# Three banks for the sums of the long mLSTM scan, one for its transposes, the next head's scores inside the round, and loads of two later stages moved

## The chip, the core and the metric

The kernel runs on one core of a Trainium2 chip, in one launch. A core has a matrix engine (TensorE, "PE" in the profile; its weight loads, which overlap the products, stand as "PEld"), a vector engine ("DVE"), a scalar engine ("ACT"), GpSimd ("POOL") and SyncE ("SP"), from whose queue nearly all DMA transfers of this kernel are issued. Matrix products go to banks of an accumulator memory (PSUM), from which ACT or DVE reads them. The metric is the time of one execution on the device, in microseconds (us).

## The reference

One encoder layer, applied to a long input of 1024 tokens and a short one of 512, both 1024 wide, with the same weights:

```python
h = rms_norm(x, pre_w)
cols = jnp.einsum('bsd,dc->bsc', h, w_in)
m_qk, m_v, m_o, m_z, m_i, m_f, a_qkv, a_z, gate = jnp.split(cols, ...)
y_m = mlstm_mixer(m_qk, m_v, m_o, m_i, m_f, ...) * silu(m_z)
y_a = dilated_attention(a_qkv, rel_table) * silu(a_z)
p_m, p_a = y_m @ w_pm, y_a @ w_pa
g = sigmoid(gate)                       # one gate per branch
merged = g[:, :, 0] * p_m + g[:, :, 1] * p_a
return x + rms_norm(merged @ w_out, post_w)
```

The mLSTM mixer has 4 heads of 256 channels and runs over chunks of 128 tokens, forward and backward; the two directions are added. In one chunk of one direction:

```python
sc = jnp.einsum('nhtk,nhsk->nhts', qc, kc) * jnp.exp(d_log - mt[..., None])
num = jnp.einsum('nhts,nhsv->nhtv', sc, vc) + wa[..., None] * jnp.einsum('nhtk,nhkv->nhtv', qc, c_mat)
h = num / jnp.maximum(jnp.abs(den), jnp.exp(-mt))[..., None]
c_new = decay[..., None, None] * c_mat + jnp.einsum('nhsk,nhsv->nhkv', kw, vc)
```

The attention has three groups (window 128 with stride 1, 512 with stride 4, 2048 with stride 16) of 8 heads of 64 channels. The groups' outputs are mixed, weighted by their softmax denominators.

## The kernel before

Every large product is made in three passes of split numbers: high by high, high by low and low by high (`mm3`, lines 194 to 196, so these three lines stand for most of PE's work). ACT makes the high half of a weight block (`split_w`, L252: `wh<-wraw`) and DVE the low half (L253: `wl`), from one of two buffers `wraw`, into one of three pairs `wh`, `wl`. One such weight block, a "unit" of 128 x 1024, serves 8 or 16 products into the banks called `dense`, three passes each. One `dense` step (called a step below) is one such triple.

The program goes through stages: the values of both inputs, then the projections of the first columns in pairs of units (up to 1056 us), the scan of the long tokens (called A; `mlstm`, to 1353), the attention of A (`attend`, to 1645), the scan of the short tokens (B; `mlstm_short`, to 1833) with the mix of A's three attention groups beside it (`combine` with `slow`), the attention of B (`attend`, to 2122), and a closing stage with the mix of B (`combine` without `slow`). All the other projections are cut into the `dense` steps, and `fill` strews them over the scans, the attentions and the closing stage: `fill(1 / 3)` gives out a third of what a round is due, by a plan that spreads a stage's number of steps (STEPS) over its calls. `fill(lead)` ahead of a stage counts as `lead` calls. The order on PE and on SP is the order of the code in these stages (`manual_schedule`); on ACT, DVE and POOL a scheduler gives the order.

**The scan of A.** `mlstm` runs 64 rounds: 4 heads, 8 chunks (`i`), 2 directions (`d`). Its PSUM pool (L870 to L872) has two banks `a` (transposes and scores), two banks `num` (the sums of a round) and one `kv` of two banks. Ahead of the rounds stand the loads of the first rows and of V, `fill(lead)`, and `prepare(0)`. `prepare(h)` is a generator of six steps for a head: twice a group of scores `a<-Q,K` (L892, 8 products of which each is in two parts, copied by ACT at L894 into `st`) and two groups of transposes of K (L901, copied by ACT at L902 back into `K`). Each takes a bank `a`.

A round `k` does: `tick()` (SP gives out `pace` queued loads and the stores that are due), one step of `prepare` of the next head where one is under way (from `i == 4` of a head on, one a round for six rounds), `rows`, `front(k + 1)` (ACT, DVE and POOL make `rm`, `sch`, `scl`, `qh`, `ql`, `kh`, `kl` for the next round's products), the `turn` of round `k - 4` (PE transposes the normed sum `hn` into a bank `a`, L1005, and DVE multiplies it into `ym`, L1007), a third of the fill, and `core(k)`. `core` multiplies the scores by V into `num`, gives a third of the fill, multiplies K by V into `kv`, a third of the fill, and multiplies `qh`, `ql` by the state `ch`, `cl` into the same `num` (six products). ACT (L990, `X<-num`, in the first four chunks) or DVE (L993, in the last four) then takes `num` over into `hacc` (an array in the buffer `X0`), which frees its bank.

**The attention** goes in 12 units. At each unit's second tile (`j == 1`) the loads of the next are queued (`ready`), and `spread(T.n - 1)` says over how many ticks they are given out; B has `T.n` = 4, A has 8. What is not yet out when the unit begins, `need` gives out at once. The scores are `lg<-V1a,Q` (L1387). In B's units V1a takes the K and Q the queries, from `aqk_b`.

**The mix** (`combine`) has per token block `t` a load of the three groups' outputs into one of two buffers (`load(t)`: `V0a`, `V1a` for B, `V0b`, `V1b` for A), `weigh`, `mix` (reads the buffer for the last time), `add`, and the `turn` of the block before. Its steps are yielded in turn to the loop beside it.

## Time and profile before

| | us |
|---|---|
| median of three runs | 2278.14 (2277.72 to 2280.95) |
| profiled execution, its own time | 2278.09 |
| its span, first to last instruction | 2276.3 |
| PE busy in it | 2235.5 |

By stage, from one answer of the trace in windows:

| stage | window, us | PE busy, us | granted clock |
|---|---|---|---|
| values of both inputs | 0 to 300 | 297.76 | 1.00 |
| pairs of units | 300 to 1056 | 753.77 | 1.00 |
| scan of A | 1056 to 1353 | 282.99 | 0.98 |
| attention of A | 1353 to 1645 | 288.35 | 1.00 |
| scan of B, mix of A | 1645 to 1833 | 186.18 | 1.00 |
| attention of B | 1833 to 2122 | 281.77 | 0.99 |
| closing stage, mix of B | 2122 to 2276 | 144.69 | 0.98 |

A window's length less PE's busy time is what PE stood still in that stage: 14.0 us in the scan of A, 7.2 in the attention of B, 9.3 in the closing stage. The granted clock is TensorE's, as a share of full speed, where 1.00 is no loss; at a lower clock the products themselves take longer, so this loss is inside the busy time. A name in the profile like `a<-Q,K` gives what an instruction writes and what it reads, without the numbers of the buffers; the order below prints some of these numbers (`wh_8712` is one of the three buffers for high halves).

### The profile page before, as it was taken

What the parts mean: (1) busy time and instruction counts of PE and PEld (TensorE: products, weight loads), DVE (VectorE), ACT (ScalarE), POOL (GpSimd) and SP (SyncE); (2) the same over time, 40 slices, a digit from 0 to 9 for tenths busy, and PEclk for the clock granted to TensorE, in tenths of its full rate; (3) what the DMA queues carried; (4) which work ended last, traced back from release to release, by engine and by line L of the source; (5) the groups of instructions that cost most, each with busy time, mean ns of one, the idle gap of its engine ahead of it and who ended that gap; (6) DMA issues with size and microseconds to landing.
All of it is one profiled execution on the core that took longest, in us unless ns stands there. A gap on an engine that the chain in (4) does not pass through costs nothing. (4 is left out here: it accounts for less than half of the span.)

```text
span 2276.3 us, 35152 instructions
## 1 busy us (share of the span) xinstructions
PE 2235.5 (98%) x12210; PEld 1951.7 (86%) x12210; DVE 1467.8 (64%) x2777; ACT 1100.5 (48%) x2255; POOL 623.6 (27%) x801
## 2 busy tenths in 40 slices
PE   9999999999999999999999999999999999999998
PEld 9999998888887888887888889989888878888787
DVE  5587556767899655643787776675477744556563
ACT  7444223434444433334677766676644354544332
POOL 1000023333333322222567640001033321311311
PEclk9999999999999999999999999999999999999999
DMA  9556435555332223424666559988788888787673
GB/s 355 192 138 143 117 113 194 196 193 195 118 111 101 95 82 109 146 97 159 242 214 218 157 164 250 237 234 216 203 240 264 250 259 221 192 261 208 219 248 116
DMA packets 253627, 425.05 MB, mean 187 GB/s; under 512 B 26209, under 2 KB 150753, under 8 KB 252681
## 3 DMA queue, kind: packets, MB, share of 16 engines
q1 hardware_dynamic: 249848, 410.20, 58.7%
q10 hardware_dynamic: 3600, 12.59, 1.4%
q8 instruction: 97, 1.59, 0.3%
q14 instruction: 82, 0.66, 0.1%
HBM read 302.72 MB, written 128.37 MB: 189 GB/s over the span
## 5 line engine op out<-in xcount | busy, mean ns | idle before, releaser
L194 PE MATMUL dense<-H,wh 128*128 128x512 f32 x672 | 280.5, 417 | 0.0
L196 PE MATMUL dense<-H,wl 128*128 128x512 f32 x672 | 265.6, 395 | 0.5 <-DVE wl L253 0.5
L195 PE MATMUL dense<-H,wh 128*128 128x512 f32 x672 | 264.5, 394 | 0.0
L196 PE MATMUL d<-Hh,phla 128*128 128x512 f32 x608 | 237.4, 390 | 2.2 <-DVE phla L538 2.2
L194 PE MATMUL d<-Hh,phla 128*128 128x512 f32 x608 | 236.9, 390 | 0.0
L195 PE MATMUL d<-Hl,phla 128*128 128x512 f32 x608 | 236.8, 390 | 0.0
L195 PE MATMUL d<-vlo,Hh 128*128 128x322 f32 x704 | 220.4, 313 | 0.8 <-DVE vlo L384 0.8
L196 PE MATMUL d<-vhi,Hl 128*128 128x322 f32 x704 | 220.3, 313 | 0.0
L194 PE MATMUL d<-vhi,Hh 128*128 128x322 f32 x704 | 220.3, 313 | 0.0
L253 DVE TENSOR_TENSOR wl<-wraw,wh 128x1024 fp32r<-128x1024 f32 x109 | 137.0, 1257 | 89.8 <-ACT wh L252 87.7
L556 POOL TENSOR_TENSOR psum_w<-pw_raw 128x512 f32<-128x512 f32 x38 | 57.5, 1512 | 445.8 <-DMA pw_raw<-w_in 422.1
L1399 DVE CUSTOM_DVE_ANT_0 ls<-lg,bias 128x256 f32<-128x256 f32 (+1 forms) x288 | 93.7, 362 | 132.7 <-PE lg L1387 68.2
L194 PE MATMUL d<-Hh,phlb 128*128 128x512 f32 x456 | 177.6, 390 | 0.0
L196 PE MATMUL d<-Hh,phlb 128*128 128x512 f32 x456 | 177.6, 389 | 0.0
L195 PE MATMUL d<-Hl,phlb 128*128 128x512 f32 x456 | 177.6, 389 | 0.0
L1403 ACT ACTIVATE ls<-ls,nm 128x256 f32<-128x256 f32 (+1 forms) x288 | 129.9, 453 | 79.6 <-DVE nm L1401 63.1
L252 ACT ACTIVATE wh<-wraw 128x1024 fp32r<-128x1024 f32 x110 | 116.0, 1054 | 85.1 <-DMA wraw<-w_pm 32.8
L196 PEld LDWEIGHTS dense<-H,wl 128*128 128x128 f32 x672 | 126.7, 189 | 29.7 <-DVE wl L253 0.9
L195 PEld LDWEIGHTS dense<-H,wh 128*128 128x128 f32 x672 | 127.8, 190 | 13.6
L194 PEld LDWEIGHTS dense<-H,wh 128*128 128x128 f32 x672 | 127.4, 190 | 13.5
L196 PEld LDWEIGHTS d<-Hh,phla 128*128 128x128 f32 x608 | 114.1, 188 | 27.6 <-DVE phla L538 4.2
L195 PEld LDWEIGHTS d<-vlo,Hh 128*128 128x128 f32 x704 | 133.5, 190 | 1.5 <-DVE vlo L384 1.4
(556 smaller groups left out, 5722.2 us busy)
## 6 DMA issues: line engine op xcount, KB each, us to landing
pw_raw<-w_in SPq DMA_DIRECT2D x76, 512.0 KB
wraw<-w_in SPq DMA_DIRECT2D x76, 512.0 KB
aqk_a<-pwk SPq DMA_DIRECT2D x48, 512.0 KB
aqk_b<-sw SPq DMA_DIRECT2D x48, 256.0 KB
wraw<-w_pm SPq DMA_DIRECT2D x24, 512.0 KB
wraw<-w_out SPq DMA_DIRECT2D x24, 512.0 KB
vb<-w_vp SPq DMA_DIRECT2D x16, 644.0 KB
va<-w_vp SPq DMA_DIRECT2D x14, 644.0 KB
```

What stands on the lines that cost most here:

```text
L194: nc.tensor.matmul(out, lh, rh, start=start, stop=False)
L195: nc.tensor.matmul(out, lh, rl, start=False, stop=False)
L196: nc.tensor.matmul(out, ll, rh, start=False, stop=stop)
L252: self.splits = (nc.scalar.activation(hi[:, :n], raw[:, :n], AF.Copy), on.tensor_sub(lo[:, :n], raw[:, :n], hi[:, :n].bitcast(F32)))
L253: on.tensor_sub(lo[:, :n], raw[:, :n], hi[:, :n].bitcast(F32)))
L556: self.nc.gpsimd.tensor_add(s[:, 0], ws[1][:, 0], ws[1][:, 1])
L1399: nc.vector.tensor_tensor_reduce(out=ls[:, hh], in0=ts["lg"][hh], in1=bt[:, hh], scale=1.0, scalar=NEG, op0=OP.add, op1=OP.max, accum_out= ...
L1403: nc.scalar.activation(ls[:, hh], ls[:, hh], AF.Exp, bias=nm[:, hh:hh + 1], accum_out=ot[:, 128 + hh:129 + hh])
```

## The change

Five things are changed.

- The scan of A has one bank `a` and three banks `num`, in place of two and two.
- A step of the next head's `prepare` is given out inside `core(k)`, after the products into `kv` and their share of the fill, ahead of the six products of `qh`, `ql`. Before, it stood at the round's start, ahead of `rows`, `front` and `turn`.
- The lead of the scan of A is 8 in place of 4.
- In `attend`, B's unit 1 has its loads given out over one tick, in place of three. All others stay.
- `combine` gives out `load(0)` and `load(1)` at its start and `load(t + 2)` after the mix of `t` (beside the scan of B) or after its sum (in the closing stage). Before, `load(t + 1)` stood ahead of block `t`'s work.

```diff
--- before.py
+++ after.py
@@ -868,7 +868,8 @@
         with ExitStack() as stack:
             sb = self.pool(stack, "ml" + T.name, 2, "right")
             ps = self.ml_ps = self.pool(stack, "ml_ps" + T.name, 2, "right", PSUM)
-            bank = {"a": lambda: ps.tile([P, 4, P], F32, name="a"), "num": lambda: ps.tile([P, 512], F32, name="num"),
+            bank = {"a": lambda: ps.tile([P, 4, P], F32, name="a", bufs=1),
+                    "num": lambda: ps.tile([P, 512], F32, name="num", bufs=3),
                     "kv": lambda: ps.tile([P, 2, 512], F32, name="kv", bufs=1)}
             spare = {b: bank[b]() for b in banks}
             psum = lambda b: spare.pop(b, None) if b in spare else bank[b]()
@@ -946,6 +947,8 @@
                     nc.vector.scalar_tensor_tensor(kl, kc, wsc, kh.bitcast(F32), op0=OP.mult, op1=OP.subtract)
                     m["k"] = (kh, kl)
 
+            coming = []
+
             def core(k):
                 h, i, d = rounds[k]
                 x, m = head[h], made.pop(k)
@@ -965,6 +968,8 @@
                     for ct in range(2):
                         self.mm3(pc[:, ct, :258], (kh[:, ct], kl[:, ct]), v, True, True)
                     fill(1 / 3)
+                for x1 in coming:
+                    next(x1, None)
                 if i > 0:
                     qh, ql = m["q"]
                     _, ch, cl = C[d]
@@ -1021,7 +1026,6 @@
             for _ in prepare(0):
                 fill(1 / 3)
             front(0)
-            coming = None
             for k, (h, i, d) in enumerate(rounds):
                 self.tick()
                 if i == (n > 4) and d == (n <= 4):
@@ -1032,9 +1036,7 @@
                         after()
                         self.spread(2 * n - 4)
                 if d == 0 and i == n // 2 and h < 3:
-                    coming = prepare(h + 1)
-                if coming is not None and next(coming, coming) is coming:
-                    coming = None
+                    coming.append(prepare(h + 1))
                 if k % 4 < 2:
                     rows(k // 4 + 1, k % 4)
                 if k + 1 < len(rounds):
@@ -1468,7 +1470,7 @@
                     if j == 1:
                         if i < 11:
                             coming = ready(i + 1)
-                            self.spread(T.n - 1)
+                            self.spread(T.n - 1 if i or T.n > 4 else 1)
                         elif after:
                             after()
                             self.spread(T.n + 1)
@@ -1556,20 +1558,23 @@
             self.put(("ym", T.S, 4), T.ym[8:12, :, t * P:(t + 1) * P].rearrange("c p s -> p c s"), ya, az)
 
         load(0)
+        load(1)
         yield
         az, w = {}, []
         for t in range(T.n):
             az[t] = az_of()
             self.fetch(("az", T.S), az[t].rearrange("p (c s) -> p c s", c=4), T.az[:, :, t * P:(t + 1) * P].rearrange("c p s -> p c s"))
-            if t + 1 < T.n:
-                load(t + 1)
-            for step in (lambda: w.append(weigh(t)), lambda: mix(t, w[t]), lambda: add(t)):
+            for i, step in enumerate((lambda: w.append(weigh(t)), lambda: mix(t, w[t]), lambda: add(t))):
                 with self.tc.issue_after(self.splits[0].ins), self.tc.issue_after(self.splits[1].ins):
                     step()
                 if slow:
                     yield
+                    if i == 1 and t + 2 < T.n:
+                        load(t + 2)
             if not slow:
                 yield
+                if t + 2 < T.n:
+                    load(t + 2)
                 yield
             if t > 0:
                 turn(t - 1, az[t - 1])
@@ -1995,7 +2000,7 @@
                 sraw = sp.tile([P, BLK + 2], F32R, name="sraw")
                 N.sg, N.sraw = Rot(N, [sraw[:, :BLK]]), sraw.bitcast(F32)
                 head = N.ml_load(A, 0)
-                N.mlstm(A, fill, STEPS[0], head, ("a", "num", "kv"), 4,
+                N.mlstm(A, fill, STEPS[0], head, ("a", "num", "kv"), 8,
                         hold("qkv", lambda: N.att_first(A)))
                 with ExitStack() as s3:
                     lanes = N.lanes_short(B, N.pool(s3, "lane2", 1, "right"), lambda: N.bank("o").rearrange("p a b -> p (a b)"))
```

What this does to the order, at three places. The first is PE at the start of the scan of A. Before, the first scores (L892) come behind the last step of the second weight unit that stands ready (`wh_8710`), and its steps go on between the groups of `prepare(0)`:

```order
L196 MATMUL dense<-H_8720,wl_8711 128x512
L194 MATMUL dense<-H_8720,wh_8710 128x512
L195 MATMUL dense<-H_8721,wh_8710 128x512
L196 MATMUL dense<-H_8720,wl_8711 128x512
L892 MATMUL a<-Q_8778,K_8779 128x128 x8
L194 MATMUL dense<-H_8720,wh_8710 128x512
L195 MATMUL dense<-H_8721,wh_8710 128x512
L196 MATMUL dense<-H_8720,wl_8711 128x512
L901 MATMUL a<-ident,K_8779 128x128 x4
L194 MATMUL dense<-H_8722,wh_8710 128x512
L195 MATMUL dense<-H_8723,wh_8710 128x512
L196 MATMUL dense<-H_8722,wl_8711 128x512
```

In the changed kernel the lead goes on through that unit and through six steps of the third, which lies in `wh_8712`, and the scores (now L893) and transposes (L902) stand behind these:

```order
L196 MATMUL dense<-H_8722,wl_8711 128x512
L194 MATMUL dense<-H_8720,wh_8712 128x512
L195 MATMUL dense<-H_8721,wh_8712 128x512
L196 MATMUL dense<-H_8720,wl_8713 128x512
L194 MATMUL dense<-H_8720,wh_8712 128x512
...
L194 MATMUL dense<-H_8722,wh_8712 128x512
L195 MATMUL dense<-H_8723,wh_8712 128x512
L196 MATMUL dense<-H_8722,wl_8713 128x512
L893 MATMUL a<-Q_8778,K_8779 128x128 x8
L902 MATMUL a<-ident,K_8779 128x128 x4
L194 MATMUL dense<-H_8722,wh_8712 128x512
```

The first scores have moved from behind 11 steps of the scan's lead to behind 22, and the last six of these use the third weight unit. ACT's order at the same place, before (`st` and `K` are the copies out of `a`, `wh` the high half of a weight unit):

```order
L938 ACTIVATE qh<-qw 128x256
L894 ACTIVATE st_8794<-a 128x512
L930 ACTIVATE sch<-rm 128x128
L902 ACTIVATE K_8779<-a 128x2x256
L945 ACTIVATE kh<-K_8779,col_382 128x256
L902 ACTIVATE K_8779<-a 128x2x256
L926 ACTIVATE rm<-rm,col_382 128x128
L894 ACTIVATE st_8794<-a 128x512
L252 ACTIVATE wh_8712<-wraw_8706 128x1024
L930 ACTIVATE sch<-rm 128x128
```

And ACT's order in the changed kernel:

```order
L939 ACTIVATE qh<-qw 128x256
L641 ACTIVATE sw_8775<-dense 128x512
L252 ACTIVATE wh_8712<-wraw_8706 128x1024
L252 ACTIVATE wh_8708<-wraw_8707 128x1024
L252 ACTIVATE wh_8710<-wraw_8706 128x1024
L895 ACTIVATE st_8794<-a 128x512
L931 ACTIVATE sch<-rm 128x128
L903 ACTIVATE K_8779<-a 128x2x256
L946 ACTIVATE kh<-K_8779,col_382 128x256
L927 ACTIVATE rm<-rm,col_382 128x128
L903 ACTIVATE K_8779<-a 128x2x256
```

The high half of the third unit, which stood behind both score copies, now stands ahead of both, with those of the two units after it.

The second place is PE in a round of the scan of A in which a `turn` follows a step of the next head's `prepare`, from the six products of `qh`, `ql` on (`ident` is the unit matrix by which PE transposes, `K_9046` the next head's K, `hn_8801` a normed sum):

```order
L194 MATMUL num<-ch_9605,qh 128x258
L195 MATMUL num<-cl_9606,qh 128x258
L196 MATMUL num<-ch_9605,ql 128x258
L194 MATMUL num<-ch_9605,qh 128x258
L195 MATMUL num<-cl_9606,qh 128x258
L196 MATMUL num<-ch_9605,ql 128x258
L901 MATMUL a<-ident,K_9046 128x128 x4
L1005 MATMUL a<-ident,hn_8801 128x128 x2
L194 MATMUL dense<-H_8722,wh_8708 128x512
L195 MATMUL dense<-H_8723,wh_8708 128x512
```

The same round in the changed kernel, where the numbers of the buffers K, `ch` and `cl` differ:

```order
L196 MATMUL dense<-H_8722,wl_8711 128x512
L902 MATMUL a<-ident,K_9085 128x128 x4
L194 MATMUL num<-ch_9645,qh 128x258
L195 MATMUL num<-cl_9646,qh 128x258
L196 MATMUL num<-ch_9645,ql 128x258
L194 MATMUL num<-ch_9645,qh 128x258
L195 MATMUL num<-cl_9646,qh 128x258
L196 MATMUL num<-ch_9645,ql 128x258
L1010 MATMUL a<-ident,hn_8801 128x128 x2
L194 MATMUL dense<-H_8722,wh_8710 128x512
```

The transposes of K have moved from behind the six products to ahead of them; the `turn` follows six products later instead of at once, and both take the one bank `a` where they took one of two. With `d` and `i` as before, each of the first three heads has such places.

The third place is SP at unit 1 of B's attention. Before, from the first of its loads on (`wraw` is a raw weight unit, `ymr` and `sraw` are inputs of a projection, `bias` the bias table, `sw` a result that is stored):

```order
L231 DMA ymr_18367<-ym_a 128x512
L231 DMA Q_18005<-aqk_b 64x512 x2
L231 DMA V1a<-aqk_b 64x512 x3
L210 DMA wraw_8706<-w_pm 128x1024
L231 DMA ymr_18368<-ym_a 128x512
L210 DMA wraw_8707<-w_pm 128x1024
L231 DMA ymr_18369<-ym_a 128x512
L231 DMA V1a<-aqk_b 64x512
L231 DMA Q_18005<-aqk_b 64x512 x2
L231 DMA V1a<-aqk_b 64x512 x2
L210 DMA aqk_b<-sw_8775 128x512
L210 DMA aqk_b<-sw_8776 128x512
...
L231 DMA sraw<-ym_a 128x512
L231 DMA V1a<-aqk_b 64x512 x2
L231 DMA bias_8768<-erep 128x256 x2
```

And in the changed kernel:

```order
L231 DMA ymr_18367<-ym_a 128x512
L231 DMA Q_18008<-aqk_b 64x512 x2
L231 DMA V1a<-aqk_b 64x512 x4
L231 DMA Q_18008<-aqk_b 64x512 x2
L231 DMA V1a<-aqk_b 64x512 x4
L231 DMA bias_8768<-erep 128x256 x2
L210 DMA wraw_8706<-w_pm 128x1024
L231 DMA ymr_18368<-ym_a 128x512
L210 DMA wraw_8707<-w_pm 128x1024
L231 DMA ymr_18369<-ym_a 128x512
L210 DMA aqk_b<-sw_8775 128x512
L210 DMA aqk_b<-sw_8776 128x512
```

All eight loads of `V1a` and four of `Q` now stand together, followed by the bias table's two, ahead of the two weight units `w_pm`, where the last two of `V1a` and the bias table stood behind three weight units and two stores.

## The prediction

> **What bounds the kernel now.** I read the page first, then the list of waits of PE, then the granted clock in windows, and last the timeline around each wait that the change can touch. Of the page, its first line and PE's; of the waits, "engine, line, what it waited for: us in total, times, longest":
>
> ```profile
> span 2276.3 us, 35152 instructions
> PE 2235.5 (98%) x12210; PEld 1951.7 (86%) x12210; DVE 1467.8 (64%) x2777; ACT 1100.5 (48%) x2255; POOL 623.6 (27%) x801
> ...
> PE num L194 <- ACT X L990: 6.8, 6, 2.3
> PE lg L1387 <- DMA sraw<-ym_a: 4.7, 1, 4.7
> PE a L892 <- DMA K<-qk_a: 3.7, 2, 2.3
> PE dense L194 <- DVE mg L1716: 2.4, 1, 2.4
> PE num L194 <- ACT rm L926: 1.3, 1, 1.3
> PE num L194 <- DVE X L993: 0.9, 2, 0.5
> ```
>
> PE is the bound: 2276.3 - 2235.5 = 40.8 us of the span is idle, and the change adds no matrix multiplication and takes none away. Only PE's waits, and what they drag behind them, can move. The largest are the four that the change is near: the sums' banks (`num`, 6.8 + 0.9), the first unit change in the short attention (4.7), the start of the long scan (3.7) and the closing stage (2.4).
>
> A wait also costs something behind it. The windows (length, busy time and count of PE, PEld, DVE, ACT, POOL, then PE's granted clock, DMA share, GB/s) show it:
>
> ```profile
> 1090.00:1100.00 10.00, 6.73 (x38) 5.28 (x38) 7.64 (x16) 6.54 (x18) 6.77 (x10) 0.97 1.00 393
> 1100.00:1110.00 10.00, 10.00 (x55) 8.99 (x54) 7.38 (x15) 6.19 (x15) 4.36 (x10) 0.86 1.03 358
> 1855.00:1865.00 10.00, 5.24 (x20) 4.22 (x20) 2.98 (x8) 5.82 (x14) 3.93 (x6) 0.66 1.02 322
> 1290.00:1300.00 10.00, 10.00 (x55) 8.94 (x55) 6.42 (x16) 6.41 (x17) 4.32 (x7) 0.83 0.90 200
> ```
>
> After a wait of 2.3 us the clock is lowered: 0.03 and 0.14 of two 10 us windows are lost, 1.7 us (0.17 of 10 in the second place, at 1290); after the wait of 4.7 us 0.34 of 10 us, part of it while PE still stood, so about 1.9 us. So **a pause over 2 us costs 1.7 to 1.9 us more**.
>
> The sum below is made against the profiled execution, 2278.09 us (its span 2276.3 and 1.8 around it), which stands at the median of the three runs, 2278.14.
>
> **The start of the long scan: +8.2 us.** Timeline rows are start, duration, engine, line, operation, and in brackets the wait before it:
>
> ```profile
> 1056.51 0.39 PE L194 MATMUL dense<-H,wh 128*128 128x512 f32 x1
> ...
> 1063.76 0.39 PE L196 MATMUL dense<-H,wl 128*128 128x512 f32 x1
> ...
> 1065.62 0.49 PE L892 MATMUL a<-Q,K 128*128 128x128 f32 x2 [1.47 <-DMA K<-qk_a]
> ...
> 1068.37 2.97 PE L892 MATMUL a<-Q,K 128*128 128x128 f32 x14 [2.26 <-DMA K<-qk_a]
> ...
> 1068.71 2.15 SPq L210 DMA_DIRECT2D wraw<-w_in  x2
> ...
> 1077.38 1.06 ACT L252 ACTIVATE wh<-wraw 128x1024 fp32r<-128x1024 f32 x1 [0.22 <-DMA wraw<-w_in]
> ...
> 1079.75 0.50 PE L196 MATMUL dense<-H,wl 128*128 128x512 f32 x1 [0.49 <-DVE wl L253]
> ...
> 1080.78 0.28 PE L194 MATMUL num<-V0a,sch 128*128 128x258 f32 x1
> ...
> 1083.07 1.06 ACT L252 ACTIVATE wh<-wraw 128x1024 fp32r<-128x1024 f32 x1 [1.14 <-DMA wraw<-w_in]
> ```
>
> Now the lead is 11 steps of three products (1056.51 to 1063.99: 0.68 us a step), then the scores wait for K until 1068.37. The change makes it 22 steps, so the wait for K goes. But two units of weights, 16 steps, are ready; they end at 1056.5 + 16 x 0.68 = 1067.4. The third unit's weights are asked of SP at 1068.71, behind the Q, K and V loads, and stay there in the order of after; they land at 1077.4 and their high half is ready at 1078.44. **PE stands from 1067.4 to 1078.5, 11 us**, where it stood 3.7. From there to the first `num` product come 12 steps (8.2), two score groups (16 products each, 2 x 1.70) and four transpose groups (4 x 0.35): 13.0. The low half, ready at 1079.75, holds the first step for 0.8, the lowered clock costs 1.3 (it ran down while PE stood), and the single bank makes five hand-overs in a row, which I put at 2.2: each waits for ACT's copy (0.58), behind which ACT has `sch`, `kh` or `rm` before the next one, against one step of 0.68 as cover. ACT's fourth split, ahead of the score copies now, ends at 1083.07 + 1.06, before they are due. So the first `num` starts at 1078.5 + 13.0 + 0.8 + 1.3 + 2.2 = 1095.8 instead of 1080.78: 15.0 later, of which 10 steps (6.8) are work done ahead. That leaves 8.2; bounds 4.7 (no hand-over waits, no lowered clock) and 11 (twice the clock's loss). The steps moved ahead leave 2.69 a round instead of 2.84, 0.1 us less cover in each round; I count nothing for it, since the rounds between the waits run without a gap.
>
> **The third bank: -7.0 us.** Two waits at a `num` bank, and beside the second what its products need:
>
> ```profile
> 1098.19 0.39 PE L194 MATMUL num<-V0a,sch 128*128 128x258 f32 x1 [2.29 <-ACT X L990]
> ...
> 1288.37 0.45 POOL L931 TENSOR_TENSOR scl<-rm,sch 128x128 fp32r<-128x128 f32 x1
> 1289.58 0.51 ACT L945 ACTIVATE kh<-K,col 128x256 fp32r<-128x256 f32 x1
> 1289.74 0.39 PE L194 MATMUL num<-V1a,sch 128*128 128x258 f32 x1 [2.32 <-ACT X L990]
> ```
>
> With a third bank a round waits for the copy of the round before last, one round (3 to 4 us) earlier. The waits are 6.8 + 0.9 = 7.7, and 3.4 of clock behind the two long ones: 11.1 at most, 0 at least. The wait of 2.29 I take whole, with its clock: 4.0. The one of 2.32 moves: `scl` ends at 1288.82 and `kh` at 1290.09, so the next products stand behind these; 0.5, and half of the clock, 0.9. Of the other 3.1, half, 1.6; together 6.5, and 0.5 for the first rounds, whose loads have 8 us more. What is late next is `scl` on POOL and `kh` on ACT.
>
> **One bank for transposes: +4.5 us.** PE's products into `a`, and ACT's copies out of it:
>
> ```profile
> 1128.25 1.95 PE L892 MATMUL a<-Q,K 128*128 128x128 f32 x16
> 1131.19 0.57 ACT L894 ACTIVATE st<-a 128x512 f32<-128x512 f32 x1
> ...
> 1204.12 0.60 PE L901 MATMUL a<-ident,K 128*128 128x128 f32 x4
> 1206.67 0.58 ACT L902 ACTIVATE K<-a 128x512 f32<-128x512 f32 x1
> ```
>
> In after the scores of the next head stand in front of the six `q` products (0.72), and `turn` of the round behind them. It comes 1.07 us after the transposes begin, or 2.4 after the scores begin; the copies end 3.13 and 3.51 after. In full this is a wait of 2.1 and 1.1. There are three such places in each of three heads: 0 to 13.4 (nine gaps between such rows as they stand now). While PE waits ACT catches up, and only the first of each three is paid nearly whole: 4.5. Behind PE stand the `dense` and `num` products, nothing else.
>
> **Loads of the short attention: -6.0 us.**
>
> ```profile
> V1a<-aqk_b SPq DMA_DIRECT2D x32, 128.0 KB
> ...
> 1848.34 1.06 ACT L252 ACTIVATE wh<-wraw 128x1024 fp32r<-128x1024 f32 x1 [2.96 <-DMA wraw<-w_pm]
> ...
> 1853.70 0.59 ACT L1413 ACTIVATE pts<-pt 128x512 f32<-128x512 f32 x1
> ...
> 1854.11 1.09 SPq L231 DMA_DIRECT2D V1a<-aqk_b  x2
> ...
> 1860.34 1.15 PE L1387 MATMUL lg<-V1a,Q 128*128 128x256 f32 x2 [4.74 <-DMA sraw<-ym_a]
> ```
>
> The scores wait for the last two `V1a` loads, issued at 1854.11 behind a row of stores and weights. (The row names another load that landed with them.) In after all fourteen loads of that unit go out in one turn, ahead of two `wraw` and two `ymr`, so the wait of 4.7 and its 1.9 of clock go: 6.6. Ten loads of 128 KB pushed ahead of `wraw` put it off by some 4 us, so the split of 1848.34 becomes 1852.4, and `pts` behind it 1854.1 to 1854.7, where PE wants it at 1854.31: 0.5 back. Bounds -6.6 and -2 (should a later split block ACT as long again).
>
> **Loads of the mix.** In the closing stage:
>
> ```profile
> V1a<-og_b SPq DMA_DIRECT2D x6, 264.0 KB
> ...
> 2126.00:2128.00 2.00, 2.00 (x11) 1.65 (x10) 1.46 (x2) 0.59 (x2) 0.26 (x1) 1.00 0.98 309
> 2131.05 1.06 ACT L252 ACTIVATE X<-wraw 128x1024 fp32r<-128x1024 f32 x1 [0.71 <-DMA wraw<-w_out]
> 2134.25 1.60 SPq L231 DMA_DIRECT2D V1a<-og_b  x3
> ...
> 2141.61 0.17 DVE L1523 TENSOR_TENSOR cw<-V1a 128x8 f32<-128x8 f32 x1 [2.34 <-DMA V1a<-og_b]
> 2143.41 0.50 PE L194 MATMUL dense<-wh,H 128*128 128x512 f32 x1 [2.38 <-DVE mg L1716]
> ```
>
> DVE stands at the mix's first row behind the load of 2134.25, and PE behind DVE: 2.4, and 1.7 of clock. Moved up, that load goes; but its three parts (264 KB each, 0.81 MB) now lie ahead of the `wraw` that ACT is already waiting for at 2131.05, and at 300 GB/s put it off by 2.7 us: PE then waits about 2.4 there, with half a chance of the clock. Net -1.0, bounds -4.1 and +3. In the mix of the long tokens the loads also move up; the weights there are two units ahead, 16 steps or 11 us, so nothing; without that cover 2.7 us.
>
> **A rule of the skill against this.** The rows above lower the clock after a pause of 2.3 us. The Trainium skill, "TensorE: Matmul & The Clock Gate", its closing table, asks only that idle gaps stay below about 3 us, one idle window of the monitor. The trace differs (2.32 us, clock 0.83 in the ten microseconds after it), so the sum goes by the trace; what the other would give stands below as a rival.
>
> **Sum**: 8.2 - 7.0 + 4.5 - 6.0 - 1.0 = -1.3, so 2278.1 - 1.3 = **2276.8 us**.
>
> **Rivals.**
> - *The single bank is paid in full* (slower). ACT's copy stays as late behind PE as now, each of the nine places costs its gap: 13.4 in place of 4.5, 2285.7 us. It decides from the point where a copy ends later than 1.07 us after its transposes begin. For it: the copy above ends 3.13 after. Against: ACT is busy 48% and gains while PE stands. Chance 0.22.
> - *The scan is freed* (faster). All 11.1 of the bank waits go, and the copies come forward, since the scheduler gives them out anew: 1 in place of 4.5. 2278.1 + 8.2 - 11.1 + 1 - 6.0 - 1.0 = 2269.2. For it: the six bank waits end at one and the same copy. Against: `scl` and `kh` above. Chance 0.30.
> - *The third bank does not do what it says*: the feeders (`kh`, `scl`, `rm`) are late anyway, as 1.3 us of the list already is, and of the 7.0 only 2 come: 2281.8. Chance 0.06.
> - *Short pauses cost no clock*: then the scan gains 4.4 for 7.0, the closing stage 0 for 1.0, and the old pause for K costs 1.7 less, so the start 9.9: 2278.1 + 9.9 - 4.4 + 4.5 - 6.0 = 2282.1. This is the rule named above; against it stands its own row. Chance 0.02.
>
> **The numbers.** The forecast has 0.40. A measurement of this kernel can tell about 0.2%, 4.6 us, from no change: the forecast, the third and the fourth rival lie within, 0.48; the second is faster, 0.30; the first slower, 0.22. The range takes in the centres of both large rivals with a little beyond, 2268 to 2287; the forecast's own, by the bounds of the start and the closing stage, is 2272 to 2282.
>
> **What would show it.** Right: PE's first product of the third unit waits about 11 us on ACT `wh` at the scan's start; `num` waits on ACT `X` fall from 6.8 below 2; `a` <- ident, `hn` (the turn) appears among PE's waits with 3 to 6 us; `lg` no longer waits in the short attention; `dense` waits on ACT or DVE `X` near 2132 instead of on `mg`. Wrong: if the wait at the start is under 6 us, the third unit's load came earlier than its place on SP says; if the turn waits over 10 us, the first rival holds; if `num` waits as before on `kh` or `scl`, the third.

## The result and the profile after

The changed kernel takes 2293.82 us (median of 4 runs, 2288.24 to 2298.39), the kernel before 2278.9 (4 runs, 2277.72 to 2280.95). The ratio is 1.0066, with a 95% interval of 1.005 to 1.0082: 15 us slower, beyond the upper end of the forecast range (2287). The profiled execution of the changed kernel, 2298.39, is the slowest of its four.

The page of the changed kernel, its first line and PE's:

```profile
span 2296.6 us, 35144 instructions
PE 2241.6 (98%) x12210; PEld 1952.5 (85%) x12210; DVE 1469.4 (64%) x2777; ACT 1101.2 (48%) x2255; POOL 617.5 (27%) x801
```

PE has the same 12210 products and stands still for 55.0 us, where it was 40.8. Its busy time is 6.1 us longer with the same work, which is lowered clock. PE's list of waits (engine, line, what it waited for: us in total, times, longest):

```profile
PE dense L194 <- ACT wh L252: 10.9, 1, 10.9
PE dense L194 <- DVE H L1657: 4.1, 1, 4.1
PE kv L194 <- DVE cf L985: 3.2, 5, 1.4
PE a L1010 <- ACT K L903: 3.0, 5, 1.2
PE a L1010 <- ACT st L895: 3.0, 3, 1.7
PE o L1424 <- ACT ot L1426: 2.5, 3, 1.0
...
PE dense L194 <- ACT X L252: 1.8, 1, 1.8
```

The waits at `num`, at `lg` and at K, the three largest before, are gone. In their place stand one of 10.9 us for the third weight unit, 6.0 of the turn at the one bank `a`, and three kinds that were not there or were small: `kv`, `o`, and in the closing stage X and H.

Where the two profiles part, by the first row of each stage on PE (us; the last column is what the stage added):

| from | to | before | after | added |
|---|---|---|---|---|
| first step of the lead | first product into `num` | 24.3 | 40.3 | 16.0, of which 6.8 is work done ahead: 9.2 |
| first product into `num` | first `lg` of A's attention | 271.1 | 264.8 | -6.3 + 6.8 = 0.5 |
| first `lg` | last `lg` of A's attention | 293.2 | 297.8 | 4.6 |
| last `lg` of A | first `lg` of B's attention | 189.6 | 189.4 | -0.1 |
| first `lg` | last `o` of B's attention | 286.5 | 282.9 | -3.6 |
| last `o` | last product on PE | 148.9 | 157.7 | 8.8 |

These rows add up to 19.4 us, and the lead begins 1.0 later; that is more than the 15 of the medians, because this one execution lies 4.6 above its kernel's median. So the start and the closing stage are what costs. The first is the term that was forecast; the second was forecast at -1.0.

The start in the trace of the changed kernel (start, duration, engine, line, operation, and in brackets the wait before it):

```profile
1069.64 11.33 SPq L210 DMA_DIRECT2D wraw<-w_in  x3
...
1078.31 1.06 ACT L252 ACTIVATE wh<-wraw 128x1024 fp32r<-128x1024 f32 x1 [5.13 <-DMA wraw<-w_in]
...
1079.41 0.80 PE L194 MATMUL dense<-H,wh 128*128 128x512 f32 x1 [10.88 <-ACT wh L252]
```

The load of the third unit is issued at the same place as before, behind the Q, K and V loads, and PE has run out of steps 10.88 us before its high half is ready. The product of 0.80 us, twice the 0.39 of a full clock, shows the clock still lowered; the granted clock was 0.50 of full speed from 1080 to 1085 us.

The closing stage before the change, SP's queue alone (`xo` are the rows of the input to which the result is added, `y_prompt` the stores of the result, `az` an input of the mix, `wraw<-w_pm` raw weight units):

```profile
2137.03 2.29 SPq L1745 DMA_DIRECT2D xo<-x_prompt  x4
...
2144.34 1.01 SPq L210 DMA_DIRECT2D y_prompt<-xo  x2
2145.44 0.41 SPq L231 DMA_DIRECT2D az<-az_b  x1
2146.35 1.56 SPq L231 DMA_DIRECT2D V0a<-og_b  x3
...
2153.78 1.64 SPq L210 DMA_DIRECT2D wraw<-w_pm  x2
```

And in the trace of the changed kernel, with the rows of DVE that matter (`mg` is half of a result, `X<-V0a,cw` the mix's reading of the buffer, `gab` the gates and `H` a product with its gate):

```profile
2149.40 0.90 SPq L1750 DMA_DIRECT2D xo<-x_prompt  x2
...
2155.11 0.69 DVE L1721 TENSOR_TENSOR mg<-dense,postw 128x512 f32<-128x512 f32 x1 [1.92 <-ACT mg L1713]
...
2159.08 1.90 DVE L1543 TENSOR_TENSOR X<-V0a,cw 128x512 f32<-128x512 f32 x3
...
2159.80 1.56 SPq L231 DMA_DIRECT2D V0a<-og_b  x3
2161.42 0.97 SPq L1750 DMA_DIRECT2D xo<-x_prompt  x2
2162.43 0.90 SPq L210 DMA_DIRECT2D y_prompt<-xo  x2
...
2168.93 1.02 SPq L1750 DMA_DIRECT2D xo<-x_prompt  x2
2170.04 1.48 SPq L231 DMA_DIRECT2D V1a<-og_b  x3
...
2172.87 1.39 SPq L210 DMA_DIRECT2D wraw<-w_pm  x2
...
2185.78 0.69 DVE L1657 SCALAR_TENSOR_TENSOR H<-gab,dense 128x512 f32<-128x512 f32 x1 [2.92 <-DMA gab<-gt_b]
```

`V0a<-og_b` is the load of block 2 into the buffer that the mix of block 0 reads. It now stands right behind that mix in the program, so on SP's queue it has passed two `xo` loads, two stores and an `az` load that stood ahead of it before, and there SP stands from 2150.3 to 2159.8 until DVE, which does `mg` first, has read the buffer. SP's own list of waits from 2120 to 2200 us has it:

```profile
SPq L231 <- DVE X L1543: 9.5, 1, 9.5
```

Behind it wait the `xo` loads, the stores of `y_prompt`, the next `xo` loads, and the two weight units `wraw<-w_pm`, issued 40.2 us behind the last `o` (2132.69). Before, the like pair was issued at 2153.78, 32.6 us behind the last `o` at 2121.15. PE pays at H, behind `gab`, which comes later still on the same queue. From the last `o` to its last product PE stands for 9.1 us in place of 3.4, and the granted clock is 0.97 in place of 0.99.

### The profile page after: what moved, and what is told of

It reads as the page before. It is cut to its first block, busy times and chain, and to the rows that moved or that the text cites. A ratio compares the mean times of both kernels' runs of the same rounds, so it can differ in the third digit from the quotient of the medians.

```text
span 2296.6 us, 35144 instructions
## 1 busy us (share of the span) xinstructions
PE 2241.6 (98%) x12210; PEld 1952.5 (85%) x12210; DVE 1469.4 (64%) x2777; ACT 1101.2 (48%) x2255; POOL 617.5 (27%) x801
## 5 line engine op out<-in xcount | busy, mean ns | idle before, releaser
L194 PE MATMUL dense<-H,wh 128*128 128x512 f32 x672 | 279.5, 416 | 10.9 <-ACT wh L252 10.9
L194 PEld LDWEIGHTS d<-vhi,Hh 128*128 128x128 f32 x704 | 133.8, 190 | 1.4 <-issue 0.8
```

The lines of the kernel that those rows point to most:

```text
L194: nc.tensor.matmul(out, lh, rh, start=start, stop=False)
```

## The experiments

Sixteen kernels were run, each in several rounds beside the kernel before on the same chip. Medians of the kernel before were 2276.3 to 2278.0 in these rounds. Single runs of one kernel lie up to 18 us apart (2279.81 to 2297.46), wider than the 3.2 seen at first, so what follows goes by medians of 5 to 12 runs and by the interval of each ratio; a difference of two medians under 2 us is not read. The changed kernel itself has 4 runs, from a round in which the kernel before stood at 2278.9, so "faster than the changed kernel" is uncertain by some 4 to 5 us; by the difference of the two ratios each such figure comes out 0.6 to 4.2 us lower, and some are given that way too.

### One part undone in the changed kernel

**The lead back at 4**

```diff
-                N.mlstm(A, fill, STEPS[0], head, ("a", "num", "kv"), 8,
+                N.mlstm(A, fill, STEPS[0], head, ("a", "num", "kv"), 4,
```

> The changed kernel with the lead of the long scan back at 4. If the start of the scan costs what the changed trace shows there (first product into num 16.0 us later, of which 6.8 is work done ahead: 9.2), this kernel is 9 us faster than the changed one, near 2284.5, its wait of 10.9 us on wh is gone and a wait of some 3.7 us on K is back. Rival: what is lost in the lead is given back later, since the steps done ahead are missing in later rounds; then it is within 3 us of the changed kernel's 2293.8.

Measured: 2286.46 us, ratio to before 1.0042 (1.0025 to 1.0058): 7.4 faster than the changed kernel. The wait on `wh` is gone, K's is back with 4.0. The theory holds, a little under its 9. By the ratios it is 5.5, which alone would not shut the rival out; the traces do: from the lead's first step to A's attention it takes 297.7 us in place of 305.1.

**The mix's loads as before**

```diff
         load(0)
-        load(1)
...
+            if t + 1 < T.n:
+                load(t + 1)
...
-                    if i == 1 and t + 2 < T.n:
-                        load(t + 2)
...
-                if t + 2 < T.n:
-                    load(t + 2)
```

> The changed kernel with the loads of both mixes where they were before. Theory: the load into a buffer that the mix has not yet read stands at the head of SP's queue, from 2150 to 2160 us in the changed trace, and xo, y_prompt and wraw wait behind it; then the closing stage, 8.8 us longer in the changed trace, is 7 to 9 us shorter here, near 2286, and the waits of 4.1 us on H and 1.8 on X go. Rival (the prediction's own term): the moved loads gain 1, so this kernel is 1 us slower than the changed one, near 2295, and the closing stage's length is due to the hour at which it begins.

Measured: 2285.57 us, ratio 1.0037 (1.0022 to 1.0052): 8.3 faster than the changed kernel. The waits on H and X are gone from PE's list, and from the last `o` to the last product it takes 146.1 us in place of 157.7. The theory holds; by the ratios the gain is 6.6.

**The short attention's loads as before**

```diff
-                            self.spread(T.n - 1 if i or T.n > 4 else 1)
+                            self.spread(T.n - 1)
```

> The changed kernel with the loads of the short attention's second unit spread over three ticks as before. Theory: they are worth the wait of 4.7 us and some clock, less 1.7 us of clock that the changed trace loses near 1895 us; this kernel is 4 to 6 us slower than the changed one, near 2298.5, and the wait of lg on a load of V1a or sraw is back. Rival: the later start of the stage already hides them; no difference, 2293.8.

Measured: 2293.58 us, ratio 1.0072 (1.0058 to 1.0085): no difference, though the wait at `lg` is back with 4.4. The number is the rival's, but its reason is not, since the later start hides nothing. In one trace of each, B's attention takes 287.2 us from the first `lg` to the last `o`, and 283.2 in the changed kernel: the 4.0 that the theory expected are there in that stage, and the medians do not show them.

**Two banks each**

```diff
-            bank = {"a": lambda: ps.tile([P, 4, P], F32, name="a", bufs=1),
-                    "num": lambda: ps.tile([P, 512], F32, name="num", bufs=3),
+            bank = {"a": lambda: ps.tile([P, 4, P], F32, name="a"),
+                    "num": lambda: ps.tile([P, 512], F32, name="num"),
```

> The changed kernel with two banks a and two banks num in the long scan, the next head's steps still inside the round. Theory: in the changed trace the turn's waits for the one bank a (7.4 us with those of the scores and transposes) and new waits at the one kv bank (4.8 us) eat what the third num bank saves (7.7 of waits and 3.4 of clock); this kernel is within 2 us of the changed one, 2292 to 2296, with waits at num of 4 to 8 us and none at a. Rival (the prediction's terms, -7.0 and +4.5): it is 2.5 us slower. Second rival: the one bank a alone is paid in full and num's waits would not come back in the new order; it is 5 us or more faster.

Measured: 2290.03 us, ratio 1.0052 (1.0037 to 1.0067): 3.8 faster than the changed kernel, so the exchange of banks seems to lose where the prediction's two terms gained 2.5, though the two intervals overlap. One trace of each shows the same size: from the lead's first step to A's attention it takes 301.3 us with two banks each and 305.1 in the changed kernel. It lies between the theory's 2 and the second rival's 5; `num` waits are back with 5.2 us.

### One part alone, and the banks taken apart

**Steps inside the round, on the kernel before**

```diff
+            coming = []
...
+                for x1 in coming:
+                    next(x1, None)
...
-            coming = None
...
-                    coming = prepare(h + 1)
-                if coming is not None and next(coming, coming) is coming:
-                    coming = None
+                    coming.append(prepare(h + 1))
```

> The kernel before with one part of the change: the next head's steps of prepare given out inside the round, behind the products into kv. Banks, lead and loads as before. The four undone parts account for 7.4, 8.3, 3.8 and 0 us of the 15 to 16 by which the changed kernel is slower, more than all of it; if they add up, this part alone is 3 to 5 us faster than before, near 2274, as a round's products get the steps as cover between kv and num. Rival: the parts do not add, and this one alone does nothing (within 1 us) or brings turn waits at the banks a and is slower by 2 us.

Measured: 2277.45 us, ratio 1.0008 (0.9998 to 1.0018). The rival: it does nothing that can be told from none.

**One bank `a`, three `num`, on the kernel before**

```diff
-            bank = {"a": lambda: ps.tile([P, 4, P], F32, name="a"), "num": lambda: ps.tile([P, 512], F32, name="num"),
+            bank = {"a": lambda: ps.tile([P, 4, P], F32, name="a", bufs=1),
+                    "num": lambda: ps.tile([P, 512], F32, name="num", bufs=3),
```

> The kernel before with one part of the change: one bank a and three banks num, the next head's steps at the round's start as before, where the turn follows the step at once. Theory: each such turn waits for ACT's copy in full, 9 places of about 2 us on the transposes and 3 on the scores' copy, 12 to 20 us, less the 7 to 11 that num's waits give back: 3 to 10 us slower than before, near 2284, with the turn's waits well over the 6.4 us of the changed kernel. Rival: the order inside the round matters little and the turn's waits stay at 6 to 7 us; then as with both, 2 to 4 us slower.

Measured: 2283.48 us, ratio 1.0029 (1.0019 to 1.0039): 6.9 slower, with 8.6 us of turn waits on K alone. With the steps at the round's start the turn waits more, as the theory has it.

**Both of these**

> The kernel before with the change of the long scan but for its lead: one bank a, three num, steps inside the round; loads as before. The prediction's terms for these make -2.5 us, 2275.6. The undone runs (banks 3.8 dearer, steps inside 3 to 5 cheaper) give 2278, within 2 us of before, with turn waits of 6 to 8 us, waits at kv of 2 to 5 and none at num. Rival: the long scan of the run with the lead of 4 was 2.3 us longer than before, which would give 2280.

Measured: 2280.75 us, ratio 1.0017 (1.0006 to 1.0028): 4.1 slower than before, and 2.7 faster than with the steps at the round's start. Neither the prediction's 2275.6 nor the 2278 of the undone runs; the rival's 2280.

**Steps inside, one bank `a`, `num` left at two**

```diff
-            bank = {"a": lambda: ps.tile([P, 4, P], F32, name="a"), "num": lambda: ps.tile([P, 512], F32, name="num"),
+            bank = {"a": lambda: ps.tile([P, 4, P], F32, name="a", bufs=1), "num": lambda: ps.tile([P, 512], F32, name="num"),
```

> The kernel before with the steps inside the round (2277.5 alone) and one bank a, num left at two. It prices the single bank by itself; beside it, the run with one bank a and three num (2280.8) prices the third num bank. Prediction's terms: +4.5 for the single bank and -7.0 for the third, so this one 2282 and the third bank's worth 7. Theory from the traces (the waits at kv took the place of num's): third bank worth 2 us or less net, so this one 2280 to 2283. Rival: the single bank costs 8 us or more and the third bank gives 5 or more of it back, 2285 or above.

Measured: 2280.35 us, ratio 1.0018 (1.0009 to 1.0026). Against 2277.45 the single bank `a` costs 2.9; against 2280.75 the third bank `num` brings nothing (0.4 the wrong way). The lists of PE's waits say why. With two banks each (steps inside):

```profile
PE num L194 <- ACT X L994: 4.2, 4, 1.9
...
PE num L194 <- DVE X L997: 2.7, 3, 2.0
...
PE a L1009 <- ACT K L902: 1.2, 2, 0.9
```

With one `a` and two `num`:

```profile
PE a L1009 <- ACT st L894: 4.7, 3, 1.7
...
PE a L1009 <- ACT K L902: 2.8, 5, 1.4
...
PE kv L194 <- DVE cf L984: 1.5, 2, 1.3
PE num L194 <- ACT X L994: 1.5, 2, 1.1
...
PE num L194 <- DVE X L997: 0.4, 1, 0.4
```

With one `a` and three `num`:

```profile
PE a L1010 <- ACT st L895: 5.0, 3, 1.9
...
PE a L1010 <- ACT K L903: 2.8, 5, 1.5
...
PE kv L194 <- DVE cf L985: 2.4, 4, 1.1
```

PE waits 7.5 us at the one bank `a`, and the waits at `num` fall from 6.9 to 1.9 with no third bank. A likely reading is that PE, standing at `a`, lets the engines behind it come up with the copies out of `num`; 2.7 of the 6.9 were waits for DVE, not for ACT, and they fell to 0.4 as well. The third bank then has 1.9 left to take away, and `kv` waits 0.9 more.

Where the losses lie in time the traces do not show. From the lead's first step to A's attention, one trace each, it takes 296.1 us with two banks each, 296.3 with one `a` and two `num`, and 293.7 with one and three. PE stands for 13.5, 16.3 and 14.9 us of it, and from the first product into `num` on the granted clock is 0.99, 1.00 and 1.00: what the single bank adds in waits comes back as clock. So in these traces the single bank costs nothing there and the third gains 2.6, where the medians say 2.9 lost and nothing gained; a worth of some 2 us for the third bank is not excluded, one of 7 is.

### The mechanisms by themselves

**The changed kernel, only the mix's first two loads up front**

```diff
+            if 0 < t < T.n - 1:
+                load(t + 1)
...
-                    if i == 1 and t + 2 < T.n:
-                        load(t + 2)
...
-                if t + 2 < T.n:
-                    load(t + 2)
```

> The changed kernel, but only the first load of the mix's second buffer stays up front; the later loads stand at the start of the next block's work, as before the change. Theory: what costs the closing stage its 8 us is the load behind the first mix, at which SP stands from 2150 to 2160 us; without it this kernel is 7 to 9 us faster than the changed one, near 2286, and the waits on H and on cw go while the 1.8 on X stays. Rival: the three parts of 264 KB ahead of wraw cost it, through the wait on X and the clock behind it; then it is within 2 us of the changed kernel.

Measured: 2283.11 us, ratio 1.0031 (1.002 to 1.0042): 10.7 faster than the changed kernel (8.0 by the ratios). SP's queue in this kernel, at the same place:

```profile
2143.41 2.19 SPq L1748 DMA_DIRECT2D xo<-x_prompt  x4
2148.61 1.01 SPq L210 DMA_DIRECT2D y_prompt<-xo  x2
...
2151.42 1.56 SPq L231 DMA_DIRECT2D V0a<-og_b  x3
...
2158.00 2.24 SPq L210 DMA_DIRECT2D wraw<-w_pm  x2
```

All four `xo` loads and the first stores stand ahead of `V0a<-og_b` again, and the two weight units are issued 30.2 us behind the last `o` (2127.80), 10.0 earlier than in the changed kernel. The windows (length, busy time and count of PE, PEld, DVE, ACT, POOL, then PE's granted clock, DMA share, GB/s) of the changed kernel:

```profile
2130.00:2160.00 30.00, 27.40 (x109) 21.88 (x108) 11.29 (x28) 9.57 (x20) 5.75 (x8) 0.89 0.58 183
2160.00:2190.00 30.00, 24.95 (x107) 19.76 (x107) 19.26 (x32) 6.38 (x11) 4.42 (x6) 0.96 0.83 263
```

And of this one:

```profile
2130.00:2160.00 30.00, 27.10 (x118) 21.52 (x117) 18.82 (x40) 9.37 (x18) 6.23 (x8) 1.00 0.92 292
2160.00:2190.00 30.00, 30.00 (x138) 24.55 (x137) 23.94 (x45) 8.45 (x11) 1.91 (x4) 1.00 0.78 264
```

In the window in which SP stands the transfers moved 183 GB/s against 292, and in the window behind it PE is busy for 24.95 us of 30 against 30.00. The windows are the same in time since the start, but this kernel's closing stage begins 4.9 us earlier; moved by that, they show 246 GB/s (2125.1 to 2155.1) and 30.00 us of PE (2155.1 to 2185.1), so the difference stands. The load of the second buffer up front still holds PE 0.8 us at X for a later `wraw`; the loads behind the mix are what costs.

**The changed kernel with the third weight unit loaded early**

```diff
+            self.flush(lambda p: p[1][0] == "w")
             self.need(("qk", 0))
             for d in range(2):
                 rows(0, d)
```

> The changed kernel with one line more: the load of the third weight unit is issued ahead of the Q, K and V loads of the long scan, so that it lands before 1060 us instead of at 1077. Theory: the changed kernel's 10.9 us at the start are the place of this load on SP, nothing else; PE's wait on wh goes, and with it the lowered clock behind it; 10 to 13 us faster than the changed kernel, 2281 to 2284, and the first product into num some 26 to 28 us after the first step of the lead instead of 40. Rival: the wait only moves to the fourth unit's weights or to K; then less than half of it comes back, 2288 or above.

Measured: 2283.03 us, ratio 1.0037 (1.0023 to 1.0051): 10.8 faster than the changed kernel (6.6 by the ratios). Its trace at the start:

```profile
1046.23 0.33 SPq L210 DMA_DIRECT2D wraw<-w_in  x1
...
1057.45 1.04 ACT L252 ACTIVATE wh<-wraw 128x1024 fp32r<-128x1024 f32 x1
...
1077.44 1.12 PE L902 MATMUL a<-ident,K 128*128 128x128 f32 x4 [3.89 <-ACT K L903]
```

The load goes out 8.4 us ahead of the lead's first step in place of 12.2 behind it, 20 us earlier, and PE no longer stands at `wh`. The first product into `num` comes 32.3 us after the lead's first step, not 26 to 28: the one bank `a` holds the transposes for 3.89 us instead. So the price of the start is the place of that load, as the theory says, and a part of what the rival says is true as well.

**On the kernel before: lead of 8 and that early load**

```diff
+            self.flush(lambda p: p[1][0] == "w")
...
-                N.mlstm(A, fill, STEPS[0], head, ("a", "num", "kv"), 4,
+                N.mlstm(A, fill, STEPS[0], head, ("a", "num", "kv"), 8,
```

> The kernel before with a lead of 8 and the third weight unit's load ahead of the scan's other loads, nothing else. Theory: the start gains 4 to 6 us (K's wait of 3.7, wl's of 0.5, clock 1.7), 2271 to 2273. Rival: the steps done ahead are missing as cover in later rounds: the scan from its first num product to its end is 2 us or more longer than before when the 11 steps (7.5 us) are counted, and the time is within 2 us of before.

Measured: 2274.07 us, ratio 0.9987 (0.9976 to 0.9998). Two banks `a`, and the first `num` comes after 27.8 us. From there to A's attention it takes 262.5 us where 271.1 less the 6.8 done ahead would be 264.3, so nothing is given back within the scan; but its profile has the wait of `lg` in B's attention at 7.1 us, longer than the 4.7 of before. In the traces the gain up to A's attention is 5.1 (295.4 to 290.3), as the theory has it, and B's attention takes 4.3 more; the time keeps 2 to 3 of it.

That wait is not a steady one: in the kernel before and the seven that give out these loads as it does, it is 3.1 to 7.1 us long, one trace each, though their edits are elsewhere. A part of what a small edit seems to gain or lose may stand there.

**That, with the steps inside and the mix's second buffer up front**

```diff
+                for x1 in coming:
+                    next(x1, None)
...
+            self.flush(lambda p: p[1][0] == "w")
...
-                N.mlstm(A, fill, STEPS[0], head, ("a", "num", "kv"), 4,
+                N.mlstm(A, fill, STEPS[0], head, ("a", "num", "kv"), 8,
...
+        load(1)
...
-            if t + 1 < T.n:
+            if 0 < t < T.n - 1:
```

> The kernel before with what the runs leave of the change: steps inside the round, a lead of 8 with the third weight unit's load ahead of the scan's other loads, the mix's second buffer loaded up front (later loads as before). Banks and the short attention's loads as before. Theory: K's wait of 3.7, the 1.7 of clock behind it and the wait of 0.5 on wl go at the start, the wait of 2.4 on mg in the closing stage: 4 to 8 us faster than before, 2269 to 2273. Rival: 11 steps taken out of the scan's rounds leave less cover there and the gain is given back within the scan, as num waits; then within 2 us of before.

Measured: 2274.94 us, ratio 0.9996 (0.9985 to 1.0007): no gain that can be told. A wait of 6.2 us at `lg` stands in its profile too, and 6.8 at `num`.

### The short attention's loads

**Alone, on the kernel before**

```diff
-                            self.spread(T.n - 1)
+                            self.spread(T.n - 1 if i or T.n > 4 else 1)
```

> The kernel before with one part of the change: the short attention's second unit has its loads given out over one tick. Theory: the wait of lg (4.7 us and 1.9 of clock) goes, but the two weight units behind the loads land later, ACT stands at the splits and the copies of o (ot) behind them, and PE waits there instead: within 2 us of before, no wait of lg on V1a or sraw, and three or more waits of o on ot between 1850 and 1885 us, 2 us or more together. Rival (the prediction's term): 4 to 6.6 us faster, and in the changed kernel it was the clock near 1895 that hid this by chance.

Measured: 2274.22 us, ratio 0.9988 (0.9977 to 0.9998): 2.1 faster, between theory and rival. In the trace B's attention is 4.0 shorter (286.8 to 282.8). The wait at `lg` is gone, and one of 1.7 us at `o` stands between 1850 and 1885 us, not three. The clearest case of that wait is in the changed kernel with the lead of 4:

```profile
1882.60 1.06 ACT L252 ACTIVATE wh<-wraw 128x1024 fp32r<-128x1024 f32 x1 [3.17 <-DMA wraw<-w_pm]
...
1884.40 0.26 ACT L1426 ACTIVATE ot<-o 128x128 f32<-128x128 f32 x1
...
1884.71 1.10 PE L1424 MATMUL o<-X,pts 128*128 128x64 f32 x8 [2.36 <-ACT ot L1426]
```

ACT stands 3.17 us at a split for a weight unit that is late, the copy of `o` stands behind it, and PE at the one bank of `o` for 2.36.

**The weight unit ahead of the loads, with the mended start**

Beside the lines of the mended start and of the one tick, both shown above, this kernel has:

```diff
+                    if j == 1 and i == 0 and T.n <= 4:
+                        self.flush(lambda p: p[1][0] == "w")
                     self.tick()
```

> The kernel before with the start of the scan mended (lead of 8, third weight unit loaded early: 2274.1), the short attention's loads given out over one tick, and the one weight unit that is due then issued ahead of them. Theory: with that unit no longer behind the loads the first split is on time, the waits of o on ot stay under 1 us until 1890 us and the loads keep their gain of 4 to 6: 2268 to 2270. Rival: the unit after it, still behind the loads, holds ACT all the same: 2273 to 2276.

Measured: 2269.26 us, ratio 0.996 (0.9948 to 0.9973): 7.0 faster than before, 4.8 than the mended start alone, and the fastest of all. The time is the theory's, but what the theory says of the trace is not there: `o` still waits 1.69 us at 1857.58.

**Two ticks**

The mended start, and:

```diff
-                            self.spread(T.n - 1)
+                            self.spread(T.n - 1 if i or T.n > 4 else 2)
```

> The kernel before with the start of the scan mended (2274.1) and the short attention's loads given out over two ticks, so that half of them stand behind two weight units and ahead of the stores and the third. Theory: weights as early as before the change, last V1a some 3 us earlier, so about half of the 6 us at lg comes back and nothing at ot: 2270 to 2272. Rival: as with one tick, what lg gains o loses at ot: 2273 to 2276.

Measured: 2271.5 us, ratio 0.9967 (0.9954 to 0.998); 5 runs. `lg` waits 0.6 and 0.2 us there, `o` 1.32. It is the theory's range, though `o` waits as well.

**The weight unit first, and the mix's second buffer up front**

> The same as the kernel with the weight unit ahead of the loads, with the mix's second buffer loaded up front and its later loads as before. Theory: the wait of 2.4 us on mg in the closing stage goes, partly for a wait on wraw: 0 to 3 us faster than that kernel, 2266 to 2270. Rival: the wait on X for the delayed wraw eats it, no difference.

Measured: 2271.27 us, ratio 0.9974 (0.9963 to 0.9985): no gain over the kernel without the mix's load (2269.26), as the rival has it: in the trace the waits at `mg` go from 2.5 to 1.0 us, and one of 1.7 at X has come.

## Why the prediction was wrong

- **The bound** was right: PE, 98% busy before and after, and only waits, and the clock behind them, moved.
- **The start, +8.2**, was right in mechanism and size: the wait was forecast as 11 us and is 10.9; the first `num` came 16.0 us later in place of 15.0, of which 2.5 us (half speed from 1080 to 1085) are lowered clock, put at 1.3. Undoing the lead gave 7.4, moving the load 10.8. (The upper bound of 11 does not follow from its words; with twice the clock's loss it is 9.5, and 9.2 lies within that too.)
- **The mix, -1.0**, is the step that failed. The prediction looked at the place of the load of 2134.25, "Moved up, that load goes", and at what lies behind it. It did not follow the loads after it, which go into a buffer that the mix has yet to read, nor name what is queued behind them on SP. What the runs showed in its place is SP standing for 9.5 us at such a load, with weights, stores and gates behind it. That costs 8.3 (undone) to 10.7 (only the later loads put back), or 6.6 to 8.0 by the ratios. The bound of +3 was the price of the bytes; what costs is SP's order.
- **The third bank, -7.0**, is a term that was mis-sized: it measured +0.4, that is, nothing that can be told (in one trace of each, 2.6 gained). The prediction counted the waits at `num` and those at `a` as two sums. They are not: with a single `a`, 1.9 of 6.9 us at `num` are left without any third bank. The prediction wrote "While PE waits ACT catches up" for the one term and did not carry it into the other. (Its items also add up to 7.0 before the last 0.5, not to 6.5.)
- **The single bank, +4.5**, measured +2.9, with two intervals that overlap; the first rival, 13.4, fell. PE's waits at the turn were 6.0 to 7.5 us, eight of them, so the wait was larger than forecast and a part of it came back elsewhere. Together the exchange of banks is a loss of 3.3 to 3.8 by the medians.
- **The short attention's loads, -6.0**, was too large: -2.1 alone, 0.2 the wrong way in the changed kernel; within the stage, in one trace of each, -4.0 both times. Its stated end of -2 ("should a later split block ACT as long again") is what was measured, and the rows at 1882 us show the mechanism in one kernel. That it accounts for all that is missing is not shown, since the kernel with the weight unit first kept such a wait and was faster.
- **The steps inside the round**, counted as nothing, measured 0.8 with an interval across zero.
- **The signs** that were to show it right came, all of them in kind: 10.9 us at `wh`, no wait at `num` on X, 6.0 at the turn, none at `lg` in the short attention, one at X. They stood at the places of the forecast's own terms, and none of them at what waits behind a moved load on SP.

Terms measured one by one: 7.4 + 0.4 + 2.9 + 0 + 8.3 + 0.8 = 19.8, where 15 was measured. Each median is uncertain by about 2, and they come from rounds on different chips. Taken by the ratios to the kernel before, at 2277 us, the same terms are 5.5 - 0.2 + 2.3 - 1.4 + 6.6 + 1.8 = 14.6, so that nothing need be missing or counted twice; the runs cannot tell the two sums apart. What the 4.6 us of A's attention in the changed profile are stays open: PE stands there 2.1 longer than before, and the granted clock is 0.99 in place of 1.00. With the lead of 4 the same stretch was 1.9 longer than before, with the loads of B's attention put back 0.8.

## What to carry to other kernels

Where one queue gives out transfers in program order, a load into a buffer still in use should stand no earlier than the point at which the buffer is free in time, because everything behind it waits for that buffer; moving a load up is worth a look at all that it is moved past. Waits of one engine at several banks are not separate sums: here PE waited longer at one and less at the next. Taking away a bank at one place and adding one at another may only move the wait. When the signs of a forecast are written down, one should stand at what a moved transfer passes, not only at what it serves. Where PE runs ahead of its weights, the place of the next weight load decides, and in the changed kernel one line that issued it 20 us earlier was worth more than the banks.

## What the runs showed of the hardware that was not expected

In the changed kernel PE waited twice within 2 us, 0.97 and 0.58 us for V1a and V1b, at 1390 us, and the clock fell behind it; a window of 5 us there:

```profile
1390.00:1395.00 5.00, 4.18 (x17) 3.47 (x18) 2.42 (x10) 2.35 (x10) 1.36 (x5) 0.72 0.85 248
```

0.28 of 5 us, 1.4 us, is lost behind pauses each of which is under half of the 2.3 us that the prediction took as the smallest pause with a price. In the profile of the kernel with the mix's loads as before the same place shows it again (0.74 for 1385 to 1390 us). PE stood for 1.9 of the 10 us from 1385 to 1395 in the changed kernel, so shorter gaps beside the two may have a part in it. The Trainium skill, "TensorE: Matmul & The Clock Gate", its closing table, puts the limit at idle gaps of about 3 us; the rows do not agree with that. Another section of that page of the Trainium skill, "A second HAM failure mode: psum-queue depth-cycling", tells of a bf16 kernel whose matrix engine idled shortly between groups of products, often enough for the clock to swing; this is nearer to what stands here, and the lost 1.4 us is the number that these runs add.
